# A split projection of 8192 rows: remaining columns by halves of K, and pairs of row tiles taken two at a time

## The chip, the cores and the metric

The kernel runs on one core of a Trainium2 chip. A core has five engines that run side by side, each with its own queue of instructions: TensorE (PE), which multiplies a stationary 128x128 tile with a moving one of up to 512 columns and adds up in PSUM; VectorE (DVE) and ScalarE (ACT), which read PSUM and write SBUF; GpSimd (POOL), which works on SBUF; and SyncE (SP), which here only issues DMA transfers. Weight loads of PE are shown on a line of their own (PEld). The metric is the device time of one execution in microseconds; the median of several runs counts.

## The reference

```python
def setup_inputs():
    batch, seq, hidden = 16, 512, 768
    x = randn(batch, seq, hidden); w_qkv = randn(hidden, 3 * hidden)      # float32

def reference(x, w_qkv):
    qkv = np.matmul(x, w_qkv)
    q, k, v = the three blocks of 768 columns
    return np.stack([q, k, v], axis=0).astype(np.float32)
```

So a matrix of 8192 x 768 is multiplied with one of 768 x 2304, and the result is stored as three matrices of 8192 x 768, in all 75.5 MB.

## The kernel before

**Tiling.** The rows are taken in 32 pairs of row tiles, p = 0 to 31, of 256 rows each (two tiles of 128). K is 768, split in two halves of 384, each three steps of 128 (`KH` = 3). Of the 2304 columns, 2048 are two column blocks of 1024, q = 0 and q = 1, and 256 are left, columns 1024 to 1279: these are "the remaining columns", `REM`.

**Quads.** A pair p and a block q make a quad: a product of 256 x 768 by 768 x 1024, seen as 2 x 2 by 2 x 2 blocks. It is computed with seven block products instead of eight (Strassen's scheme in Winograd's form). `product` (L233 to L247) issues one of them as three matmuls of 512 columns. Products 1 and 2 take x rounded to bfloat16 (`xb`) and weights in bfloat16 (`b1`). Products 3 to 7 take sums of blocks of x (`s`) and of the weights (`t`, `b22`) in float32r. `do` (L255 to L282) issues a product and what follows it. Product 1 starts the bank u.x, and ACT copies it to the output tile (L253). Product 2 goes to a bank of its own, u.z, and DVE adds it to that copy (L266). Product 6 is added to u.x and copied by ACT (L269). Product 5 starts the bank u.y. Product 7 is added to u.x, ACT copies it (L275) and DVE adds u.y (L276). Product 4 is added to u.x and copied by ACT (L279). Product 3 is added to u.y, and DVE adds that to an output block (L282). So u.x lives from product 1 to product 4, and u.y from product 5 to product 3. PSUM has eight banks, from one pool.

**The remaining columns.** `rem_row` (L297) issues six matmuls of 256 columns for one row tile, over all six steps of K, with x and weights in bfloat16 (`w_rem[0]` for the first half of K, `w_rem[1]` for the second). `rem` does both row tiles of a pair in one bank, and returns a function that has ACT copy the bank (L313), which returns one that stores it from SP (L314).

**Preparing x.** `load_x` loads a pair with four DMAs, two by SP and two by the queue it is given. `transpose` (L148) turns it on DVE, in one instruction of 128x1536 or in `parts`. `round_x` makes `xb` on POOL (L191), and `sums_x` makes the five blocks of `s` on POOL (L211 to L215). `ahead(p)` does the three in that order. The pools hold 3 loaded pairs, 2 transposed, 4 rounded, 2 of sums, 5 output tiles (of 128x2048, two row tiles by one block), and one more output-sized tile, "both", which the startup uses for weights and then for the quad of p = 2, q = 1.

**Startup.** For p = 0 and 1 everything is plain bfloat16 products (`block`), while the weights arrive. Between the second block and the first quad come the remaining columns of p = 0 and 1, the first four row tiles (`rems = [rem(p) for p in range(2)]`, L529). Their weights come with two DMAs from POOL (L419), one for each half of K, that round float32 to bfloat16 on the way. ACT's order there is: two copies of block results, rounding of the first row tile of p = 2 (L200), copy of p = 0's remainder (L313), two more block results (L446), rounding of the second row tile (L200), copy of p = 1's remainder (L313), then the copy of product 1 of the quad p = 2, q = 0 (L253). p = 2's quads follow, the first of them among the blocks.

**Steady part.** From p = 3 to 30 each pair is one call of `two(a, b, early)`, whose order is written out by hand: product 1 of both quads; `early`, which prepares p + 1 and loads p + 2; the pair's remainder; product 2 of both; then products 6, 6, 5, 7, 5, 7 of a, b, a, a, b, b, then 4 and 3 of a, its store, 4 and 3 of b, its store. A store of a quad is two DMAs on SP of 768 KB and 256 KB (L289, L290, L293, L294). The load of p + 2 goes half through SP and, from p = 5 on, half through ACT's queue.

**Last pair.** `last` takes p = 31 and stores by blocks of columns as they are ready (`store_cols`, L354), nine DMAs on SP and three on ACT. The first row tile's remainder comes after a's product 4, the second one's at the very end, each stored by ACT's queue (L370).

Instructions of an engine run in the order in which the program gives them. The framework adds the semaphore waits; a tile of a pool is handed out again when all that used it are done.

Of the kernel before, what the change touches and what calls it, by code (L numbers as in the profile page):

```python
# [10 lines left out]
def kernel(  # L11
# [20 lines left out]
    nc = tc.nc  # L32
    P = 128
    G = 32
# [5 lines left out]
    KH = KT // 2  # L40
    KC = K // 4
    NP = M // (2 * P)
    CB = 512
    REM = N3 - 4 * CB
    Q_OFF = (0, 2 * CB + REM)
    R_OFF = 2 * CB
    fp32 = mybir.dt.float32
# [13 lines left out]
    bt_pool = ctx.enter_context(tc.tile_pool(name="bt", bufs=1))  # L61
# [9 lines left out]
    ps_pool = ctx.enter_context(tc.tile_pool(name="ps", bufs=8, space=bass.MemoryType.PSUM))  # L71
# [5 lines left out]
    w_rem = [w_pool.tile([P, KH, REM], bf16, name="w_rem0"), None]  # L77
# [6 lines left out]
    both = bt_pool.tile([P, 2, KH * CB], fp32, name="both", tag="both")  # L84
# [37 lines left out]
    xin, xf, xb, sr = {}, {}, {}, {}  # L122
# [19 lines left out]
    def load_x(p, other):  # L142
        xin[p] = xin_pool.tile([P, 2 * P // G, KC], fp32, name="xin")
        load_x_half(p, 0, nc.sync)
        if other is not None:
            load_x_half(p, 1, other)

    def transpose(p, parts=1):  # L148
        t = xf_pool.tile([P, KT, 2 * P], fp32, name="xf")
        turned = t[:].rearrange("p j (g b) -> p g j b", b=G)  # L150
        rows = xin.pop(p)[:].rearrange("p g (a j) -> p g j a", a=G)
        n = 2 * P // G // parts
        for g in range(0, 2 * P // G, n):
            nc.vector.transpose(turned[:, g:g + n], rows[:, g:g + n])  # L154
        xf[p] = t

# [30 lines left out]
    def round_x(p):  # L189
        xb[p] = xb_pool.tile([P, KT, 2 * P], bf16, name="xb", tag="xb")  # L190
        nc.gpsimd.tensor_copy(out=xb[p][:], in_=xf[p][:])  # L191
# [12 lines left out]
    def sums_x(p, eng=None):  # L204
        t = xf.pop(p)
        a11, a12 = t[:, :KH, :P], t[:, KH:, :P]
        a21, a22 = t[:, :KH, P:], t[:, KH:, P:]
        s = s_pool.tile([P, 5, KH, P], f32r, name="s")
        sr[p] = s
        sums = {  # L210
            1: lambda g: g.tensor_tensor(s[:, 1], a21, a22, op=add),  # L211
            2: lambda g: g.tensor_tensor(s[:, 2], s[:, 1], a11, op=sub),  # L212
            3: lambda g: g.tensor_tensor(s[:, 3], a11, a21, op=sub),  # L213
            0: lambda g: g.tensor_copy(out=s[:, 0], in_=a22),
            4: lambda g: g.tensor_tensor(s[:, 4], a12, s[:, 2], op=sub),  # L215
        }
        if eng is not None:
            return sums
        for n in (1, 2, 3, 0, 4):
            sums[n](nc.gpsimd)  # L220
# [5 lines left out]
    def quad(p, q, pool=o_pool, tag="o"):  # L226
        u = Quad()
        u.p, u.q = p, q
        u.o = pool.tile([P, 2, 2 * CB], fp32, name="o", tag=tag)
        u.x = u.y = u.z = None  # L230
        return u
# [17 lines left out]
    def bank():  # L249
        return ps_pool.tile([P, CB], fp32, name="ps")  # L250

    def evacuate(u):
        nc.scalar.activation(u.o[:, 0, :CB], u.x[:], ident)  # L253

    def do(u, n, out=True):  # L255
        c11, c12 = u.o[:, 0, :CB], u.o[:, 0, CB:]
        c21, c22 = u.o[:, 1, :CB], u.o[:, 1, CB:]
        if n == 1:
            u.x = bank()
            product(u, 1, u.x, True)  # L260
            if out:
                evacuate(u)
        elif n == 2:
            u.z = bank()
            product(u, 2, u.z, True)
            nc.vector.tensor_tensor(c11, c11, u.z[:], op=add)  # L266
        elif n == 6:
            product(u, 6, u.x, False)
            nc.scalar.activation(c12, u.x[:], ident)  # L269
        elif n == 5:  # L270
            u.y = bank()
            product(u, 5, u.y, True)
        elif n == 7:
            product(u, 7, u.x, False)
            nc.scalar.activation(c22, u.x[:], ident)  # L275
            nc.vector.tensor_tensor(c22, c22, u.y[:], op=add)  # L276
        elif n == 4:
            product(u, 4, u.x, False)
            nc.scalar.activation(c21, u.x[:], ident)  # L279
        elif n == 3:  # L280
            product(u, 3, u.y, False)
            nc.vector.tensor_tensor(c12, c12, u.y[:], op=add)  # L282
# [4 lines left out]
    def store_quad(u):  # L287
        if u.q == 0:
            nc.sync.dma_start(rows_of(0, u.p, 0, H), u.o[:, :, :H])  # L289
            nc.sync.dma_start(rows_of(1, u.p, 0, 2 * CB - H), u.o[:, :, H:])  # L290
        else:
            part = 2 * H - Q_OFF[1]
            nc.sync.dma_start(rows_of(1, u.p, H - part, H), u.o[:, :, :part])  # L293
            nc.sync.dma_start(rows_of(2, u.p, 0, H), u.o[:, :, part:])  # L294


    def rem_row(p, r, ps):  # L297
        for j in range(KT):
            nc.tensor.matmul(  # L299
                ps, xb[p][:, j, r * P:(r + 1) * P], w_rem[j // KH][:, j % KH, :],  # L300
                start=(j == 0), stop=(j == KT - 1), skip_group_check=True,
            )

    def rem(p, eng=nc.sync, between=None):
        ps = ps_pool.tile([P, 2, REM], fp32, name="ps")
        rem_row(p, 0, ps[:, 0, :])
        if between is not None:
            between()
        rem_row(p, 1, ps[:, 1, :])

        def copied():
            o = or_pool.tile([P, 2, REM], fp32, name="orem")
            act.activation(o[:], ps[:], ident)  # L313
            return lambda: eng.dma_start(rows_of(1, p, R_OFF - H, R_OFF - H + REM), o[:])  # L314

        return copied

    def two(a, b, early, u=None):

        do(a, 1)  # L320
        do(b, 1, u is None)
        if u is None:
            early()
            rem(a.p)()()
        else:
            middle(u)
            copied = rem(a.p, between=lambda: third(u))
            evacuate(b)
            early()
            copied()()  # L330
            fourth(u)
        do(a, 2)
        do(b, 2)
        do(a, 6)
        do(b, 6)
        do(a, 5)
        do(a, 7)
        do(b, 5)
        do(b, 7)
        do(a, 4)  # L340
        do(a, 3)
        store_quad(a)
        do(b, 4)
        do(b, 3)
        store_quad(b)

    def store_cols(u, r, lo, hi, eng):

        c = Q_OFF[u.q] + lo
        end = Q_OFF[u.q] + hi  # L350
        while c < end:
            n = min(end, (c // H + 1) * H)
            row = (2 * u.p + r) * P
            eng.dma_start(  # L354
                out_flat[c // H, row:row + P, c % H:c % H + n - c],
                u.o[:, r, c - Q_OFF[u.q]:n - Q_OFF[u.q]],
            )
            c = n

    def last(a, b):  # L360

        p = a.p

        def rem_stored(r):
            ps = bank()
            rem_row(p, r, ps[:, :REM])
            o = or_pool.tile([P, 2, REM], fp32, name="orem")
            nc.scalar.activation(o[:, 0, :], ps[:, :REM], ident)  # L368
            row = (2 * p + r) * P
            nc.scalar.dma_start(out_flat[1, row:row + P, R_OFF - H:R_OFF - H + REM], o[:, 0, :])  # L370

        do(a, 1)
        do(b, 1)
        do(a, 2)
        do(a, 6)
        do(b, 2)
        do(b, 6)
        for u in (a, b):
            store_cols(u, 0, 0, CB, nc.sync)
        for u in (a, b):  # L380
            do(u, 5)
            do(u, 7)
            store_cols(u, 1, CB, 2 * CB, nc.sync)
        do(a, 4)
        store_cols(a, 1, 0, CB, nc.scalar)
        rem_stored(0)
        do(b, 4)
        store_cols(b, 1, 0, CB, nc.scalar)
        for u in (a, b):
            do(u, 3)  # L390
            store_cols(u, 0, CB, 2 * CB, nc.sync)
        rem_stored(1)


    ND = 2
# [21 lines left out]
    for h in range(2):  # L417
        rows = w_qkv.rearrange("(p j) n -> p j n", j=KT)[:, h * KH:(h + 1) * KH]
# [17 lines left out]
    quads = {}  # L436
# [49 lines left out]
    def ahead(p):  # L486
        transpose(p)
        round_x(p)
        sums_x(p)
# [7 lines left out]
    turned = [turn_row(0, 0)]  # L497
# [28 lines left out]
    late = block(  # L526
        0, 1, bt, [((j, ), range(4)) for j in range(KH)] + [(range(KH, KT), range(4))]
    )
    rems = [rem(p) for p in range(2)]  # L529
    transpose(2, 2)  # L530

    late[0]()
# [22 lines left out]
    u = quad(2, 0)  # L555
# [42 lines left out]
    u2 = quad(2, 1, bt_pool, "both")  # L598
    do(u2, 1)
    do(u2, 2)  # L600

    for p in range(ND + 1, NP):
        def early():
            if p + 1 < NP:
                ahead(p + 1)
            if p + 2 < NP:
                load_x(p + 2, nc.sync if p <= ND + 2 else nc.scalar)

        a, b = quad(p, 0), quad(p, 1)
        if p == ND + 1:  # L610
            two(a, b, early, u2)
        elif p < NP - 1:
            two(a, b, early)
        else:
            last(a, b)


# [28 lines left out]
```

## Time and profile before

| | us |
|---|---|
| median of 3 runs | 360.74 (360.47 to 361.23) |
| the profiled execution, its own time | 361.78 |
| its span, first to last instruction | 360.0 |
| PE idle before the first remainder on the second half of K, until the weights' DMA | 0.6 (by the page's ends of matmuls) |
| median from issue to landing, a quad's 768 KB store | 4.6 |
| the same, a quad's 256 KB store | 4.0 |
| the same, a load of x by SP / by ACT | 6.9 / 4.3 |

The span is that of one profiled execution, and what lies around it adds to its time. The granted clock of PE was 1.000 over the whole span. The DMA engines were busy for 90% and more of most slices of the span, at 299 GB/s on average. A line of the timeline has the start in us, the time that it spans, the engine, the source line, the operation, the tiles written and read, the shape, and the number of instructions merged; in brackets stands the idle time before it and what ended that.

### The profile page before, as it was taken

How to read it: one execution, taken by the hardware profiler on the slowest of the kernel's cores; microseconds unless marked ns; L12 is line 12 of the kernel's file. 1: busy time of each engine (PE TensorE's matmuls, PEld its weight loads, DVE VectorE, ACT ScalarE, POOL GpSimd, SP SyncE). 2: the span in 40 equal slices, each digit the busy share in tenths (PEclk: the TensorE clock that was granted, in tenths of full speed). 3: DMA queues.
4: the chain of work that ended last, by engine and by line, in shares of the span. 5: the costliest groups of instructions: out<-in, count | busy, mean ns of one | idle time of the engine just before them, and what ended most of it. 6: DMA issues, size and time to landing. Idle time of an engine off the chain costs nothing.

```text
span 360.0 us, 5248 instructions
## 1 busy us (share of the span) xinstructions
PE 351.5 (98%) x1749; PEld 251.4 (70%) x1780; DVE 227.8 (63%) x244; ACT 185.9 (52%) x316; POOL 178.8 (50%) x187
## 2 busy tenths in 40 slices
PE   7999999999999999999999999999999999999995
PEld 3465577777777777777777777777777777777764
DVE  2789676766566675566675566675556676556643
ACT  5469744545454545454545444455444445545443
POOL 0221856446664445665445665444665444665420
PEclk9999999999999999999999999999999999999999
DMA  7999999799998999899999899998999999989767
GB/s 265 340 367 345 325 357 371 236 333 298 275 325 301 295 276 290 282 319 301 292 285 284 284 309 309 292 285 282 290 295 315 293 295 272 297 283 322 291 238 257
DMA packets 82106, 107.73 MB, mean 299 GB/s; under 512 B 5408, under 2 KB 62240, under 8 KB 82080
## 3 DMA queue, kind: packets, MB, share of 16 engines
q1 hardware_dynamic: 66672, 96.35, 82.5%
q10 hardware_dynamic: 14608, 10.65, 8.9%
q0 software_dynamic: 800, 0.39, 0.8%
q8 instruction: 14, 0.23, 0.3%
q14 instruction: 12, 0.10, 0.1%
HBM read 32.28 MB, written 75.50 MB: 299 GB/s over the span
## 4 chain that ended last, share of the span: by engine, by line
PE 92%; DMA 5%; issue 1%; ACT 1%; ACTq 0%; POOL 0%; SPq 0%
PE ps L244 78%; PE ps L299 11%; PE ps L456 3%; DMA w_rem<-in_w_qkv_dram 2%; DMA xin<-in_x_dram 2%; DMA st<-in_w_qkv_dram 1%; ACT o L279 0%; ACTq L354 0%; POOL w_rem L419 0%; SPq L163 0%; ACT orem L368 0%; POOL mark L414 0%; ACTq L370 0%; ACTq L368 0%
## 5 line engine op out<-in xcount | busy, mean ns | idle before, releaser
L244 PE MATMUL ps<-t,s 128*128 128x512 f32 x720 | 181.2, 399 | 0.0
L244 PEld LDWEIGHTS ps<-t,s 128*128 128x128 f32 x720 | 135.0, 188 | 30.7
L191 POOL CAST xb<-xf 128x1536 bf16<-128x1536 f32 x28 | 41.0, 1464 | 132.2 <-DVE xf L154 132.2
L276 DVE TENSOR_TENSOR o<-o,ps 128x512 f32<-128x512 f32 x58 | 39.9, 688 | 91.5 <-ACT o L275 91.5
L154 DVE STREAM_TRANSPOSE xf<-xin 128x1536 f32<-128x1536 f32 (+1 forms) x32 | 88.7, 2775 | 1.7 <-DMA xin<-in_x_dram 1.7
L244 PE MATMUL ps<-b,xb 128*128 128x512 bf16 x331 | 85.3, 380 | 1.5
L244 PEld LDWEIGHTS <-xb 128*128 128x128 bf16 x360 | 32.8, 98 | 37.3 <-issue 7.6
L269 ACT ACTIVATE o<-ps 128x512 f32<-128x512 f32 x60 | 36.0, 600 | 43.6 <-PE ps L244 40.9
L275 ACT ACTIVATE o<-ps 128x512 f32<-128x512 f32 x58 | 34.7, 599 | 44.2 <-PE ps L244 44.2
L282 DVE TENSOR_TENSOR o<-o,ps 128x512 f32<-128x512 f32 x60 | 41.3, 688 | 21.4 <-PE ps L244 20.2
L244 PE MATMUL ps<-b,s 128*128 128x512 f32 x180 | 50.4, 389 | 0.0
L279 ACT ACTIVATE o<-ps 128x512 f32<-128x512 f32 x60 | 35.9, 598 | 24.6 <-PE ps L244 21.7
L253 ACT ACTIVATE o<-ps 128x512 f32<-128x512 f32 x60 | 35.8, 597 | 24.4 <-DVE o L282 20.7
L299 PE MATMUL ps<-w_rem,xb 128*128 128x256 bf16 x384 | 47.5, 273 | 0.6 <-DMA w_rem<-in_w_qkv_dram 0.6
L299 PEld LDWEIGHTS <-xb 128*128 128x128 bf16 x384 | 37.2, 98 | 12.3 <-issue 1.8
L266 DVE TENSOR_TENSOR o<-o,ps 128x512 f32<-128x512 f32 x60 | 37.8, 672 | 2.0 <-ACT o L253 1.3
L244 PEld LDWEIGHTS ps<-b,s 128*128 128x128 f32 x180 | 33.8, 188 | 7.1
L211 POOL TENSOR_TENSOR s<-xf 128x384 fp32r<-128x384 f32 x29 | 30.9, 1065 | 0.0
L212 POOL TENSOR_TENSOR s<-s,xf 128x384 fp32r<-128x384 f32 x29 | 29.4, 1015 | 2.3
L213 POOL TENSOR_TENSOR s<-xf 128x384 fp32r<-128x384 f32 x29 | 29.5, 1017 | 0.0
L215 POOL TENSOR_TENSOR s<-xf,s 128x384 fp32r<-128x384 f32 x29 | 29.5, 1017 | 0.0
L313 ACT ACTIVATE orem<-ps 128x512 f32<-128x512 f32 x31 | 18.5, 598 | 21.0 <-PE ps L299 21.0
(45 smaller groups left out, 119.3 us busy)
## 6 DMA issues: line engine op xcount, KB each, us to landing
out_dram<-o SPq DMA_DIRECT2D x62, 768.0 KB, 4.6
out_dram<-o SPq DMA_DIRECT2D x65, 256.0 KB, 4.0
xin<-in_x_dram SPq DMA_DIRECT2D x62, 192.0 KB, 6.9
xin<-in_x_dram ACTq DMA_DIRECT2D x50, 192.0 KB, 4.3
out_dram<-orem SPq DMA_DIRECT2D x31, 256.0 KB, 5.8
st<-in_w_qkv_dram SPq DMA_DIRECT2D x11, 256.0 KB, 5.6
st<-in_w_qkv_dram SPq DMA_DIRECT2D x3, 768.0 KB, 9.2
xin<-in_x_dram SPq DMA_DIRECT2D x4, 384.0 KB, 4.7
```

The lines of the kernel that those rows point to most:

```text
L154: nc.vector.transpose(turned[:, g:g + n], rows[:, g:g + n])
L191: nc.gpsimd.tensor_copy(out=xb[p][:], in_=xf[p][:])
L211: 1: lambda g: g.tensor_tensor(s[:, 1], a21, a22, op=add),
L244: nc.tensor.matmul(ps[:], lhs[j], rhs[j], start=(start and j == 0), stop=(j == KH - 1), skip_group_check=True,)
L253: nc.scalar.activation(u.o[:, 0, :CB], u.x[:], ident)
L266: nc.vector.tensor_tensor(c11, c11, u.z[:], op=add)
L269: nc.scalar.activation(c12, u.x[:], ident)
L275: nc.scalar.activation(c22, u.x[:], ident)
L276: nc.vector.tensor_tensor(c22, c22, u.y[:], op=add)
L279: nc.scalar.activation(c21, u.x[:], ident)
L282: nc.vector.tensor_tensor(c12, c12, u.y[:], op=add)
L299: nc.tensor.matmul(ps, xb[p][:, j, r * P:(r + 1) * P], w_rem[j // KH][:, j % KH, :], start=(j == 0), stop=(j == KT - 1), skip_group_check= ...
```

## The change

It has two parts and what they need.

**The remaining columns of p = 0 and 1 by halves of K.** A new function `rems_by_halves` takes two banks at once, and runs all four row tiles over the first half of K (12 matmuls), then all four over the second (12). The rest of `rem` is split off as `rem_copied`.

**Groups of two pairs from p = 6 on.** `group(p)` takes p and p + 1 together: product 1 of both quads of p, remainder of p, product 2 of both, then the same for p + 1, and only then products 3 to 7 of the quads of p (`rounded`, the second half of the former `two`), and those of p + 1. Preparation is placed by hand: `sums_x(p + 1)`, `transpose(p + 2)` and `round_x(p + 2)` after the first two products, `transpose(p + 3)` and `round_x(p + 3)` after the last product 2, `sums_x(p + 2)` after the first pair's float32r products. All loads of x go through SP. The first quad of a group takes the tile "both". In the last group the float32r products of p = 31 and its remainder are in `last`, which has lost its products 1 and 2.

**The way there.** For p = 3 to 5 `two` stays. Loads run further ahead (p = 3 loads 5 and 6, p = 4 loads 7, p = 5 loads 8 and 9), and in p = 5 the transpose for p = 7 is made in two halves that are put between the last products, followed by its rounding.

```diff
-    def transpose(p, parts=1):
+    def transpose(p, parts=1, split=False):
...
+        turns = [
+            lambda g=g: nc.vector.transpose(turned[:, g:g + n], rows[:, g:g + n])
+            for g in range(0, 2 * P // G, n)
+        ]
         xf[p] = t
+        if split:
+            return turns
+        for turn in turns:
+            turn()
...
+    def rems_by_halves(pairs):
+        banks = [ps_pool.tile([P, 2, REM], fp32, name="ps") for _ in pairs]
+        for h in range(2):
+            for p, ps in zip(pairs, banks):
+                for r in range(2):
+                    for j in range(KH):
+                        nc.tensor.matmul(
+                            ps[:, r, :], xb[p][:, h * KH + j, r * P:(r + 1) * P],
+                            w_rem[h][:, j, :], start=(h == 0 and r == 0 and j == 0),
+                            stop=(h == 1 and j == KH - 1), skip_group_check=True,
+                        )
+        return [rem_copied(p, ps) for p, ps in zip(pairs, banks)]
...
         do(a, 2)
         do(b, 2)
+        rounded(a, b, turns)
+
+    def rounded(a, b, turns=()):
+
         do(a, 6)
         do(b, 6)
         do(a, 5)
         do(a, 7)
         do(b, 5)
         do(b, 7)
+        for t in turns[:1]:
+            t()
         do(a, 4)
         do(a, 3)
         store_quad(a)
+        for t in turns[1:]:
+            t()
         do(b, 4)
         do(b, 3)
         store_quad(b)
...
-        do(a, 1)
-        do(b, 1)
-        do(a, 2)
-        do(a, 6)
-        do(b, 2)
-        do(b, 6)
         for u in (a, b):
             store_cols(u, 0, 0, CB, nc.sync)
+            do(u, 6)
...
-    rems = [rem(p) for p in range(2)]
+    rems = rems_by_halves(range(2))
...
+    def group(p):
+
+        quads = [quad(p, 0, bt_pool, "both"), quad(p, 1)]
+        do(quads[0], 1)
+        do(quads[1], 1)
+        sums_x(p + 1)
+        if p + 2 < NP:
+            transpose(p + 2)
+            round_x(p + 2)
+        if p + 4 < NP:
+            load_x(p + 4, nc.sync)
+        rem(p)()()
+        do(quads[0], 2)
+        do(quads[1], 2)
+        quads += [quad(p + 1, q) for q in range(2)]
+        do(quads[2], 1)
+        do(quads[3], 1)
+        if p + 5 < NP:
+            load_x(p + 5, nc.sync)
+        if p + 2 < NP:
+            rem(p + 1)()()
+        do(quads[2], 2)
+        do(quads[3], 2)
+        if p + 3 < NP:
+            transpose(p + 3)
+            round_x(p + 3)
+        rounded(*quads[:2])
+        if p + 2 < NP:
+            sums_x(p + 2)
+            rounded(*quads[2:])
+        else:
+            last(*quads[2:])
+
+    NG = ND + 4
+    extra = {NG - 3: (NG, ), NG - 1: (NG + 3, )}
+    for p in range(ND + 1, NG):
+        late_turns = []
+
         def early():
-            if p + 1 < NP:
-                ahead(p + 1)
-            if p + 2 < NP:
-                load_x(p + 2, nc.sync if p <= ND + 2 else nc.scalar)
...
+            ahead(p + 1)
+            for n in (p + 2 + (p > NG - 3), ) + extra.get(p, ()):
+                load_x(n, nc.sync)
+            if p == NG - 1:
+                late_turns.extend(transpose(NG + 1, 2, True))
+
+        two(quad(p, 0), quad(p, 1), early, u2 if p == ND + 1 else None, late_turns)
+        if p == NG - 1:
+            round_x(NG + 1)
+    for p in range(NG, NP, 2):
+        group(p)
```

More of the change, by code (lines that the diff above doesn't have):

```diff
@@ L152, in transpose @@
         n = 2 * P // G // parts
-        for g in range(0, 2 * P // G, n):
-            nc.vector.transpose(turned[:, g:g + n], rows[:, g:g + n])
+        turns = [
+            lambda g=g: nc.vector.transpose(turned[:, g:g + n], rows[:, g:g + n])
+            for g in range(0, 2 * P // G, n)
+        ]
         xf[p] = t
+        if split:
+            return turns
+        for turn in turns:
+            turn()
     def load_row(p, r):
@@ L309, in rem, with rem_copied @@
         rem_row(p, 1, ps[:, 1, :])
+        return rem_copied(p, ps, eng)
+    def rem_copied(p, ps, eng=nc.sync):
         def copied():
@@ L316, in rem, with two @@
         return copied
-    def two(a, b, early, u=None):
+    def rems_by_halves(pairs):
[10 more added lines that the diff above has]
+        return [rem_copied(p, ps) for p, ps in zip(pairs, banks)]
+    def two(a, b, early, u=None, turns=()):
         do(a, 1)
@@ L600 @@
     do(u2, 2)
-    for p in range(ND + 1, NP):
-        def early():
-            if p + 1 < NP:
-                ahead(p + 1)
-            if p + 2 < NP:
-                load_x(p + 2, nc.sync if p <= ND + 2 else nc.scalar)
[L609 to L615, printed above, removed]
+    def group(p):
[33 more added lines that the diff above has]
+        late_turns = []
+        def early():
+            ahead(p + 1)
[8 more added lines that the diff above has]
+        group(p)
 _INS = ['x', 'w_qkv']
```

## The prediction

> **What bounds the kernel now.** I read the page first: the span, the engines' busy time, and the chain that ended last.
>
> ```profile
> span 360.0 us, 5248 instructions
> ...
> PE 351.5 (98%) x1749; PEld 251.4 (70%) x1780; DVE 227.8 (63%) x244; ACT 185.9 (52%) x316; POOL 178.8 (50%) x187
> ...
> PE 92%; DMA 5%; issue 1%; ACT 1%; ACTq 0%; POOL 0%; SPq 0%
> ```
>
> TensorE (PE) is the bound, so the change can gain only where PE waits, where a matmul is slower than its neighbours, or before PE's first and after its last work. Next the chain in order of time, in the middle of the run.
>
> ```profile
> 111.94 9.16 PE ps L244 x40
> 121.10 1.31 PE ps L299 x12
> 122.68 9.16 PE ps L244 x40
> ```
>
> Pairs are counted from p = 0 to 31. A pair of row tiles takes 122.68 - 111.94 = 10.74 us, and PE has no idle time in it. What should it take? The timeline of PE gives the spacing of each sort of matmul (busy time less the last one's own, over the number less one, or start to start).
>
> ```profile
> 34.47 5.34 PE L456 MATMUL ps<-both,xb 128*128 128x512 bf16 x24
> ...
> 161.23 0.84 PE L244 MATMUL ps<-t,s 128*128 128x512 f32 x3
> 161.91 0.84 PE L244 MATMUL ps<-b,s 128*128 128x512 f32 x3
> ```
>
> bf16 of 512 columns: (5.34 - 0.38)/23 = 0.2157 us (0.38 is the mean of one). float32r: (161.91 - 161.23)/3 = 0.2267. bf16 of 256 columns, for the remaining columns: the startup rows below, (2.45 - 0.27)/20 = 0.109. A pair has 30, 12 and 12 of float32r, bf16-512 and bf16-256: 6.80 + 2.59 + 1.31 = 10.70. So 0.04 us of each 10.74 is lost, and it can only lie at the two changes of type, into float32r and out of it. That is what grouping can save.
>
> **Grouping, steady part.** The pairs p = 6 to 31 become 13 groups. Each saves one change into float32r and one out of it: 0.04 us. The last group saves two such rounds, because `last` also loses its alternation of products 2 and 6. 14 x 0.043 = -0.60 us. Bounds -0.5 to -0.7 from the rounding of the spacings.
>
> The rest of the group must stay hidden behind PE's 21.4 us. I place its work on a clock that starts with the group: bf16 work until 7.8 (four times 1.31 for products 1 and 2 with two remainders of 1.31), float32r of the first pair to 14.6, of the second to 21.4.
> - POOL: `sums_x(p+1)` needs only its buffer, free at 0; its five steps take 4.5 (1.0 each, the copy 0.5): done at 4.7, needed at 14.6. `round_x(p+2)` (1.46) 6.2, needed at 21.4. `round_x(p+3)` after the second transpose, 13.1, needed at 25. `sums_x(p+2)` from 14.7 to 19.3, needed at 29. Nothing here is near. If POOL's cover were gone each us past its time would cost PE a us per group; the nearest is 2 us away (19.3 against the next group's transpose into that buffer at 21.4+0.8).
> - DMA issues: the loads of x leave ACT's queue for SP's: eight loads, eight quad stores, two remainder stores per group. Rows give 0.4 to 1.2 us for an issue, so 7 to 22 us of 21.4; the loads land far ahead (issued by 12, first read at 22). Behind a blocked SP issue wait only stores, whose buffers are written again 5 us or more after landing. Cost 0.
> - Output buffers: three of five are used per group and "both" for the first quad; "both" is stored at about 14.3 and 15, lands in the 4.6 us of its row, and is written at 22. Cost 0.
> - VectorE (DVE) is the tight one:
>
> ```profile
> 152.65 2.94 DVE L154 STREAM_TRANSPOSE xf<-xin 128x1536 f32<-128x1536 f32 x1
> 155.51 1.25 DVE L266 TENSOR_TENSOR o<-o,ps 128x512 f32<-128x512 f32 x2
> 159.34 0.69 DVE L276 TENSOR_TENSOR o<-o,ps 128x512 f32<-128x512 f32 x1 [2.58 <-ACT o L275]
> ```
>
> Now the transpose runs at the start of a pair, long before L276. In a group the second transpose comes after the fourth product 2, hence into the start of float32r work at 155.76 on this clock: the last L266 starts 0.22 after it (as L282 does after its matmul), the transpose at 0.83, L276 at 0.83 + 2.86 = 3.69 instead of 159.34 - 155.76 = 3.58. So L276 of the first quad is 0.11 us later; product 3 overwrites what it reads and its weight load is due at 4.56, L276 ends at 4.38. Slack about 0.15. Cost 0, with a rival below.
>
> **Into the groups.** In pair p = 5 the transpose for p = 7 is put in two halves (1.4 to 1.6 each) among the last products; the second ends some 9.3 after the float32r start, `round_x(7)` 1.5 later at 10.8, and PE wants it at 6.8 + 3.9 = 10.7. +0.1 us once, 0 to 0.3. The extra loads in p = 3 and p = 5 fall into a stretch in which DMA is 90% busy and delay stores by 2 to 4 us; the buffer of p = 3's first quad is next written 10 us after its store. Cost 0.
>
> **The remainders by halves.** The startup on PE and on ACT:
>
> ```profile
> 19.80 0.49 PE L299 MATMUL ps<-w_rem,xb 128*128 128x256 bf16 x3
> 20.87 2.45 PE L299 MATMUL ps<-w_rem,xb 128*128 128x256 bf16 x21 [0.58 <-DMA w_rem<-in_w_qkv_dram]
> ```
>
> ```profile
> 22.05 0.60 ACT L313 ACTIVATE orem<-ps 128x512 f32<-128x512 f32 x1 [0.60 <-PE ps L299]
> 22.55 1.08 ACT L446 ACTIVATE o<-ps 128x512 f32<-128x512 f32 x2
> 23.50 0.86 ACT L200 ACTIVATE xb<-xf 128x768 bf16<-128x768 f32 x1
> 24.23 0.61 ACT L313 ACTIVATE orem<-ps 128x512 f32<-128x512 f32 x1
> 24.71 0.62 ACT L253 ACTIVATE o<-ps 128x512 f32<-128x512 f32 x1
> ```
>
> Three matmuls use the first half of the weights, then PE waits until 20.87 for the second: 20.87 - 19.80 - 3 x 0.109 = 0.74 us. With 12 matmuls on the first half PE gets to the second at 21.11, after it landed: the wait is gone. But ACT then works without a gap from 22.05 to L253's end, 25.33, and the first float32r product (25.77 now) must not start before L253 has read its bank. The first pair's remainder ends only 0.09 earlier (21.11 + 0.65 = 21.76 against 21.85), so L253 ends at 25.24; with the release and a float32r weight load of 0.19, PE starts at 25.53. Gain 0.24, and 0.5 is moved into a wait for ACT. Bounds 0 and -0.74; I take -0.24 since L253 is the next thing late. After that DVE, ACT and POOL have half a us or more in hand at each row that PE follows. (The Trainium skill, "TensorE: Matmul & The Clock Gate", Architectural detail, says that a matmul can begin before its weight load completes; by it the 0.19 falls away and the gain is 0.43. The page of the profile has 188 ns for such a load and shows no start from standstill, so it is open.)
>
> **The end.** This term speaks against the change. Bytes in the last stretch:
>
> ```profile
> 345.60:352.00 6.40, 6.40 (x30) 4.48 (x29) 2.47 (x4) 2.99 (x5) 0.00 (x0) 1.00 1.03 397
> 352.00:354.30 2.30, 2.30 (x15) 1.77 (x14) 0.74 (x2) 1.58 (x3) 0.00 (x0) 1.00 0.45 156
> 354.30:358.70 4.40, 1.85 (x12) 1.14 (x10) 1.37 (x2) 0.98 (x2) 0.00 (x0) 1.00 0.97 355
> ...
> DMA packets 3104, 4.46 MB, mean 262 GB/s; under 512 B 288, under 2 KB 2080, under 8 KB 3104
> ```
>
> The last two numbers of a row are the DMA share and GB/s. From 343 on, 4.46 MB are stored: the quads of p = 30 and all of p = 31. They begin at 345.6, 1.8 us after p = 30's first quad has its product 3 (343.8), and pause around 353 because PE has not made more; the last matmul streams until 355.97, the last bytes leave at 358.7, 2.7 later. In the changed kernel products 1 and 2 of p = 31 and their 2.6 us lie before those stores, not between: from that product 3 to PE's end are 6 + 30 float32r and 12 small matmuls, 8.16 + 1.31 = 9.47 us, so bytes begin 7.67 before the end. At 397 GB/s 4.46 MB take 11.23: they end 3.56 after PE, 0.9 later than now. Bounds: 410 GB/s, the most in a busy window of this trace, +0.5; 355 throughout, +2.2. I take +0.9, the rate of the window most like it. (ACT issues 0.79 MB of these. By the Trainium skill, "DMA: Bandwidth & Descriptors", Issuing engines are not separate DMA queues, they share the engines with SP's; the trace agrees, 355 with both at work. Otherwise 3.67 MB would end 1.6 after PE, the term would be 0 and the time 360.0.)
>
> **Sum.** -0.60 - 0.24 + 0.1 + 0.9 = +0.16 us. The profiled execution took 361.78 (span 360.0 and 1.78 around it), 1.04 above the median of the runs, 360.74. It becomes 361.94; the median 360.9. A measurement of this kernel can tell about 0.2%, 0.72 us, from no change: below 360.02 is faster, above 361.46 slower.
>
> **Rivals.**
> - *Product 3 waits for DVE in each group* (slower). Place: L276 of the first quad; price (delay - 0.15) x 13; it decides once the second transpose starts over 1 us into the float32r work. Half an addition late (0.35) makes 0.2 x 13 = 2.6: 363.5. For: only 0.15 us in hand. Against: POOL beside a transpose doesn't stretch it (1.58 us for a half with and without POOL at work in the startup), and its buffer is free 4 us ahead.
> - *The end drains at 355 GB/s*: +1.3 on the forecast, 362.2. For: both queues and 1 KB rows give that now. Against: most of the backlog is 3 KB rows.
> - *Startup gives all 0.74 and the end costs 0 to 0.5* (faster): -0.6 - 0.74 + 0.1 + 0 to 0.5 = -1.2 to -0.7, 359.5 to 360.0. For: the w_rem wait does vanish. Against: ACT's gapless chain, and bytes that have to move.
> - *It does not do what it says*: eight PSUM banks, of which four are held by products 1; if the third product 2 got the bank that a remainder still holds, PE would wait 0.8 a group (ACT's copy of 0.6 and its release), 13 x 0.8 = +10, 371. Against: in a pair now product 2 follows a remainder without a wait, so another bank is handed out.
>
> **How the numbers follow.** Forecast 0.50, faster rival 0.19, drain 0.13, DVE 0.15, banks 0.03. So same 0.50, faster 0.19, slower 0.31. The range, 360.0 to 362.6, holds the forecast, the drain and the near parts of the DVE case and of the faster one; the forecast's own is 360.2 to 361.4.
>
> **What would show it.** Steady groups of 21.44 us; no PE idle for w_rem, but one before the first float32r product; DMA share near 1 from PE's end less 7.7 to its end plus 3.6. Wrong would be any idle time of PE that repeats each 21.4 us, or a last landing as soon after PE as now.

## The result and the profile after

| | before | after |
|---|---|---|
| median of 6 runs, us | 360.99 (360.47 to 361.75) | 362.58 (362.3 to 362.9) |
| ratio after / before, 95% interval | | 1.0041 (1.003 to 1.0052) |
| profiled execution, us | 361.78 | 362.9 |
| its span, us | 360.0 | 361.1 |

The changed kernel is 0.41% slower, 1.1 to 1.9 us by the interval. The page of the changed kernel, in the same three lines as before:

```profile
span 361.1 us, 5246 instructions
...
PE 353.5 (98%) x1780; PEld 252.2 (70%) x1780; DVE 230.9 (64%) x245; ACT 186.1 (52%) x316; POOL 178.4 (49%) x187
...
PE 94%; DMA 3%; ACT 1%; SPq 0%; issue 0%; ACTq 0%
```

PE is still the bound, so the answer lies again in the three stretches of the prediction. The steady part, in the chain of the changed kernel (start, us, what; a group is counted here from its first remainder, 1.31 us):

```profile
185.20 1.31 PE ps L305 x12
186.51 2.59 PE ps L250 x12
189.10 1.31 PE ps L305 x12
190.41 16.26 PE ps L250 x72
206.67 1.31 PE ps L305 x12
```

206.67 - 185.20 = 21.47 us for a group, where two pairs took 21.48 and 21.44 was forecast. Nearly the whole gain of grouping is missing, with PE working without a gap. DVE in the same group shows what is late (L272 and L282 are the former L266 and L276):

```profile
191.15 1.34 DVE L272 TENSOR_TENSOR o<-o,ps 128x512 f32<-128x512 f32 x2 [2.47 <-PE ps L250]
192.40 3.07 DVE L154 STREAM_TRANSPOSE xf<-xin 128x1536 f32<-128x1536 f32 x1
195.41 0.63 DVE L282 TENSOR_TENSOR o<-o,ps 128x512 f32<-128x512 f32 x1
```

The float32r work of this group starts at 191.54 (its second matmul's start less one spacing; the first one's record begins earlier, while the last bfloat16 matmul still runs). The transpose starts 0.86 after that and lasts 3.07, not 2.94, so L282 ends at 4.50 instead of the 4.38 worked out. Product 3 has to wait for it. Its weight load, due at 4.56, starts at 4.61, 0.12 after L282's end (196.036 to 196.152 in the trace):

```profile
196.15 0.60 PEld L250 LDWEIGHTS ps<-b,s 128*128 128x128 f32 x3
```

From there six float32r matmuls follow each other at 0.228 to 0.236 us instead of 0.227, in all 0.03 us more. These are slower matmuls and no idle time. The other slow stretch of a group is at its change from bfloat16 to float32r, where the first matmuls lose 0.025 us, as they do in each pair of the kernel before; the change back costs 0.003. This is most of the 0.04 us that the prediction put there.

The startup of the changed kernel, on PE, and what PE waited for between 24 and 26 us (waiting engine and line, releaser, us in total, times, longest):

```profile
19.70 2.78 PE L333 MATMUL ps<-w_rem,xb 128*128 128x256 bf16 x24
...
25.29 1.65 PE L250 MATMUL ps<-t,s 128*128 128x512 f32 x6
```

```profile
PEld ps L250 <- ACT o L259: 0.4, 1, 0.4
PEld L305 <- ACT xb L206: 0.2, 1, 0.2
```

The wait for w_rem is gone: all 24 matmuls run in one stretch. In its place PE waits 0.4 us for L259, the copy that the prediction named (L253 before), and 0.2 for the rounding of the second row tile. From the first remainder to the first float32r product it is now 25.29 - 19.70 = 5.59 us, before 25.69 - 19.80 = 5.89. To the second float32r matmul it is 5.92 and before 6.20.

The end (the last two numbers are the DMA share and GB/s), and the instruction traffic from 343 us on:

```profile
347.80:354.00 6.20, 6.20 (x32) 4.96 (x31) 1.85 (x3) 3.37 (x6) 0.00 (x0) 1.00 1.03 397
354.00:359.40 5.40, 1.72 (x11) 1.04 (x9) 1.37 (x2) 0.98 (x2) 0.00 (x0) 0.85 1.03 371
359.40:361.10 1.70, 0.00 (x0) 0.00 (x0) 0.00 (x0) 0.00 (x0) 0.00 (x0) 0.50 0.01 2
...
q14 instruction: 1, 0.01, 0.1%
```

PE's last matmul starts at 355.45 and is counted to 355.56, one spacing later. The DMA engines are full from 347.8 on without a pause, and the last bytes leave at 359.56: 4.0 us after PE, before 2.7. From there to the end of the span it takes another 1.56, before 1.26. A q14 line, instruction memory being loaded, was not there in the same stretch of the kernel before.

From the first float32r product to the end of the span the changed kernel takes 361.1 - 25.3 = 335.8 us, the kernel before 360.0 - 25.7 = 334.3. The loss of 1.5 us lies there. The end alone has 4.0 - 2.7 + 1.56 - 1.26 = 1.6, so what lies between gives nothing in sum.

### The profile page after: what moved, and what is told of

Same layout as the page of the kernel before. It is cut to its first block, busy times and chain, and to the rows that moved or that the text cites. A ratio compares the mean times of both kernels' runs of the same rounds, so it can differ in the third digit from the quotient of the medians.

```text
span 361.1 us, 5246 instructions
## 1 busy us (share of the span) xinstructions
PE 353.5 (98%) x1780; PEld 252.2 (70%) x1780; DVE 230.9 (64%) x245; ACT 186.1 (52%) x316; POOL 178.4 (49%) x187
## 4 chain that ended last, share of the span: by engine, by line
PE 94%; DMA 3%; ACT 1%; SPq 0%; issue 0%; ACTq 0%
PE ps L250 78%; PE ps L305 10%; PE ps L481 6%; DMA xin<-in_x_dram 2%; DMA out_dram<-o 1%; PE ps L333 1%; SPq L169 0%; ACT orem L322 0%; ACT o L471 0%; ACT xb L206 0%; ACT o L285 0%; PE ps L190 0%; ACT xc L173 0%; ACT o L259 0%; ACT orem L398 0%
## 5 line engine op out<-in xcount | busy, mean ns | idle before, releaser
L250 PE MATMUL ps<-t,s 128*128 128x512 f32 x720 | 178.2, 395 | 0.1
L250 PEld LDWEIGHTS ps<-t,s 128*128 128x128 f32 x720 | 134.9, 188 | 30.1 <-ACT o L259 0.4
L154 DVE STREAM_TRANSPOSE xf<-xin 128x1536 f32<-128x1536 f32 (+1 forms) x33 | 91.0, 2760 | 1.9 <-DMA xin<-in_x_dram 1.9
L250 PE MATMUL ps<-b,xb 128*128 128x512 bf16 x360 | 85.3, 380 | 0.0
L282 DVE TENSOR_TENSOR o<-o,ps 128x512 f32<-128x512 f32 x58 | 39.4, 679 | 60.0 <-ACT o L281 60.0
L250 PEld LDWEIGHTS <-xb 128*128 128x128 bf16 x360 | 33.9, 98 | 37.1 <-issue 4.2
L272 DVE TENSOR_TENSOR o<-o,ps 128x512 f32<-128x512 f32 x60 | 38.8, 678 | 31.1 <-PE ps L250 17.4
L259 ACT ACTIVATE o<-ps 128x512 f32<-128x512 f32 x60 | 35.8, 597 | 32.0 <-PE ps L250 17.4
L250 PE MATMUL ps<-b,s 128*128 128x512 f32 x180 | 50.6, 390 | 0.0
L305 PE MATMUL ps<-w_rem,xb 128*128 128x256 bf16 x360 | 44.6, 273 | 0.0
L305 PEld LDWEIGHTS <-xb 128*128 128x128 bf16 x360 | 34.8, 98 | 11.2 <-issue 0.8
L250 PEld LDWEIGHTS ps<-b,s 128*128 128x128 f32 x180 | 33.7, 188 | 7.3
```

The costliest lines, as they stand in the source:

```text
L154: lambda g=g: nc.vector.transpose(turned[:, g:g + n], rows[:, g:g + n])
L250: nc.tensor.matmul(ps[:], lhs[j], rhs[j], start=(start and j == 0), stop=(j == KH - 1), skip_group_check=True,)
L305: nc.tensor.matmul(ps, xb[p][:, j, r * P:(r + 1) * P], w_rem[j // KH][:, j % KH, :], start=(j == 0), stop=(j == KT - 1), skip_group_check= ...
```

## The experiments

Times are medians against the kernel before on the same chip; the ratio is what counts, since the kernel before itself has 360.99 to 361.4 us from one set of runs to the next.

**The startup part alone.** The kernel before with `rems_by_halves`:

```diff
-    rems = [rem(p) for p in range(2)]
+    rems = rems_by_halves(range(2))
```

> The kernel before with the first part of the change alone. If the wait for the second half of the remainders' weights is what is saved and ACT's chain keeps the rest of it, the first float32r product starts 0.24 to 0.40 us earlier than in the kernel before (25.69 in its profile) and the time falls by as much: about 360.7. Rival: ACT's chain, or a startup that differs from run to run, takes all of it: no change, 361.0.

Measured 360.94 against 361.4, ratio 0.999 (0.9981 to 0.9999). The first float32r product came at 24.69, a whole microsecond earlier, but the first remainder had come 0.63 earlier too, which the change can't do: the time up to there differs from run to run. Between the two marks it took 5.53 us. The same in the other kernels of this study that have this startup gives 5.49 to 5.64; the kernel before has 5.88 and, in a second profile, 5.98. So the part is worth 0.2 to 0.5 us by these profiles, 0.4 in the middle, about half of the wait that it removes (0.74 in one profile and 0.82 in the other).

**A second profile of the kernel before**, for that comparison.

> The kernel before once more, for a second profile. If the startup takes another time in each run, its first float32r product is not at 25.69 us again but some tenths from it, the pairs take 10.74 us and the last bytes leave 2.7 us after PE's last matmul as before; all theories expect the same here.

The first float32r product was at 25.50, the pairs took 10.74 us, and the last bytes left 2.71 us after PE. 361.57 us in its one run.

**The second transpose earlier.** The changed kernel with one block moved ahead of the last two products 2:

```diff
+        if p + 3 < NP:
+            transpose(p + 3)
+            round_x(p + 3)
         if p + 2 < NP:
             rem(p + 1)()()
         do(quads[2], 2)
         do(quads[3], 2)
-        if p + 3 < NP:
-            transpose(p + 3)
-            round_x(p + 3)
```

> The changed kernel with the second transpose of a group put ahead of its last two products 2. If DVE's lateness at the first quad's product 3 makes the second slow stretch of float32r matmuls, that stretch is gone and a steady group takes 21.44 us instead of 21.467 (two of twelve 21.50): 0.03 to 0.05 us a group, 0.4 us in all, 362.2. Rival: POOL's rounding, which starts 0.57 us before the stretch, makes it; it now runs at the start of the float32r work, the loss moves there, a group stays at 21.47 and the time at 362.6.

The chain of this kernel, then DVE in a later group (with the weight load of product 3) and in the very first group:

```profile
185.79 1.31 PE ps L305 x12
187.10 2.59 PE ps L250 x12
189.69 1.31 PE ps L305 x12
191.00 16.23 PE ps L250 x72
207.23 1.31 PE ps L305 x12
```

```profile
192.08 1.25 DVE L272 TENSOR_TENSOR o<-o,ps 128x512 f32<-128x512 f32 x2
195.71 0.69 DVE L282 TENSOR_TENSOR o<-o,ps 128x512 f32<-128x512 f32 x1 [2.38 <-ACT o L281]
196.70 0.64 PEld L250 LDWEIGHTS ps<-b,s 128*128 128x128 f32 x3
```

```profile
81.98 1.25 DVE L272 TENSOR_TENSOR o<-o,ps 128x512 f32<-128x512 f32 x2
84.67 3.10 DVE L154 STREAM_TRANSPOSE xf<-xin 128x1536 f32<-128x1536 f32 x1 [1.43 <-POOL s L221]
87.69 1.24 DVE L272 TENSOR_TENSOR o<-o,ps 128x512 f32<-128x512 f32 x2
```

A steady group takes 207.23 - 185.79 = 21.44 us, the forecast of the prediction to 0.01, and L282 now waits for ACT (the bracket) with DVE idle before it. The weight load of product 3 starts when it is due, 4.56 us into the float32r work. The rival fell: the rounding now starts 0.09 us into that work instead of 3.99, and no loss came with it, since the first matmuls there lose 0.026 us, against 0.025 without it. But the kernel as a whole got no faster: 363.5, ratio 1.0059 (1.0047 to 1.0072), and from the first float32r product to the end of the span 336.2 us against 335.8. The expectation overlooked the first group. There the transposes of the pair before it are still in DVE's queue, the buffer is not free, the early transpose waits 1.43 us for POOL, and the additions behind it come late at product 3: that group lost 0.8 us, more than the eleven others gained.

**The rounding alone, put later.** As a check on the same rival, only `round_x(p + 3)` was put behind `rounded(*quads[:2])`.

> The changed kernel with only POOL's rounding of p + 3 put behind the first pair's float32r products. If DVE's lateness makes the second slow stretch, it stays where it is, at the first quad's product 3 (4.56 us into the float32r work), with no rounding near it; a group takes 21.47. Rival, POOL: the stretch is gone from there and appears 0.57 us after the rounding's new start, some 7 us into the float32r work.

A group took 21.47 us as before, and the slow stretch stayed where product 3 of the first quad begins (one run, 362.59 us). But the rounding stayed too. POOL has no other work between the old place and the new one, so it still rounds as soon as the transpose is done, 4.04 us into the float32r work against 3.99. This run therefore says nothing about the rival. What speaks against POOL is the kernel above, where the rounding did move, and the next one, where it keeps its place and the loss follows L282.

**DVE later still.** Four small fills behind the second transpose:

```diff
             transpose(p + 3)
             round_x(p + 3)
+            pad = m_pool.tile([P, 96], fp32, name="pad")
+            for _ in range(4):
+                nc.vector.memset(pad[:], 0.0)
```

> The changed kernel with four small DVE fills behind the second transpose of each group, which make DVE 0.4 to 0.7 us later at the first quad's product 3; nothing of the computation changes. If PE waits there and has no slack left, each group grows by that delay, to 21.9 to 22.2 us. Rival, the recorded slack of 0.15 us is there and the stretch has another cause: the group grows by 0.25 to 0.55.

DVE and PE in one group of it:

```profile
129.94 3.07 DVE L154 STREAM_TRANSPOSE xf<-xin 128x1536 f32<-128x1536 f32 x1
132.99 0.81 DVE L655 MEMSET pad<- 128x96 f32 x4
133.72 1.22 DVE L282 TENSOR_TENSOR o<-o,ps 128x512 f32<-128x512 f32 x2
```

```profile
128.90 5.13 PE L250 MATMUL ps<-t,s 128*128 128x512 f32 x21
134.49 0.93 PE L250 MATMUL ps<-b,s 128*128 128x512 f32 x3 [0.46 <-DVE o L282]
```

The fills put L282 0.77 us later, and the group takes 22.17 to 22.21 us, 0.70 to 0.74 more; the one run took 372.09 us. Now PE stands idle in front of product 3 (L250 with `b`), released by L282. The rounding still starts at 3.99, and from L282's end to the weight load it takes 0.12 again. So the changed kernel had next to no slack at that place: of 0.77 us of delay, 0.70 to 0.74 are lost in each group.

**The last two pairs one at a time.** The changed kernel with groups up to p = 29 and the old end:

```diff
-    for p in range(NG, NP, 2):
+    for p in range(NG, NP - 2, 2):
         group(p)
+    p = NP - 2
+    two(quad(p, 0), quad(p, 1), lambda: sums_x(p + 1))
+    last(quad(p + 1, 0), quad(p + 1, 1))
```

(with products 1 and 2 back in `last`.)

> The changed kernel with the last two pairs taken one at a time, as in the kernel before (p = 30 with its stores before products 1 and 2 of p = 31). If the bytes stored at the end are the cost, the last bytes leave 2.7 us after PE's last matmul instead of 3.9, and the time falls by 1.1 to 1.5: about 361.2. Rival, the loss is in the steady groups: no more than 0.1 of it comes back, 362.5.

Measured 362.01, ratio 1.0016 (1.0007 to 1.0025): 0.9 us of the loss came back, less than expected. The last bytes left 3.2 us after PE, not 2.7, and the rest to the end took 1.77 instead of 1.26, with the same stores as in the kernel before. Here too instruction memory was loaded in the last microseconds. In this run every group had the longer loss at product 3, 21.50 us.

**A group of the last two pairs alone.** The counterpart, `NG = NP - 2` in the changed kernel, with loads past p = 31 left out.

> The changed kernel with pairs up to p = 29 and a group of p = 30 and 31 alone. If the end is what made the change slower, this has all of its cost and none of the other groups': last bytes 3.9 us after PE's last matmul against 2.7, time 1.2 to 1.5 above the startup part alone, ratio to the kernel before 1.003. Rival, the 13 groups make the loss: ratio 0.999.

Measured 362.01 against 361.12, ratio 1.0026 (1.0016 to 1.0037). Its last stretch:

```profile
347.10:358.90 11.80, 8.24 (x43) 6.29 (x41) 3.43 (x5) 4.37 (x9) 0.00 (x0) 1.00 1.01 378
358.90:360.30 1.40, 0.00 (x0) 0.00 (x0) 0.00 (x0) 0.00 (x0) 0.00 (x0) 0.57 0.00 0
```

The last bytes left 3.69 us after PE, 0.97 later than in the kernel before, and the rest took 1.45, 0.2 more. No instruction block was loaded there, though here too all loads go through SP. So the stores alone cost 1.16 us, and the interval holds that less the 0.4 of the startup. The rival, that the 13 groups make the loss, fell: this kernel has only one and keeps most of it.

**The mended groups.** Earlier transpose in all groups but the first, and the last two pairs one at a time.

> The changed kernel with the second transpose earlier in all groups but the first, and the last two pairs one at a time. If the two losses are DVE's lateness and the stores at the end, steady groups take 21.44 us, the last bytes leave 2.7 to 3.2 us after PE's last matmul, and the time is that of the kernel before less 0.36 for the startup, less 0.04 x 10 for the groups, plus 0.1 on the way into them: 0.6 less, ratio 0.998. Rival: groups cost something else as well, and the ratio is no lower than that of the startup part alone, 0.999.

Groups took 21.44 us, but the ratio was 1.0013 (1.0004 to 1.0022): a miss. The end again: last bytes 3.19 after PE and 1.78 to the end. Instruction traffic from 341 us on:

```profile
q8 instruction: 1, 0.02, 0.4%
q14 instruction: 2, 0.02, 0.3%
```

The first of the two q14 blocks, of 8 KB each, is loaded 1.4 us before the last bytes, the second 1.5 us after them. The kernel before this one with the last two pairs one at a time has the same two.

**The same with ACT's loads back.** All that differs is who issues half of each load of x:

```diff
-            load_x(p + 4, nc.sync)
+            load_x(p + 4, nc.scalar)
...
-            load_x(p + 5, nc.sync)
+            load_x(p + 5, nc.scalar)
```

> The mended groups with half of each load of x issued by ACT again, as in the kernel before. If an 8 KB instruction block that is fetched on a DMA engine during the last stores (as SP's longer list of issues makes it fall there) costs 0.5 us of the last bytes and 0.5 after them, it falls elsewhere now: last bytes 2.7 us after PE's last matmul and 1.3 to the end, 1.0 less than the mended groups, ratio to the kernel before 0.998. Rival: the fetch stays in the end, or is not the cause, and the last bytes leave 3.2 us after PE's last matmul; ratio 1.001.

Measured 360.39 against 361.17, ratio 0.9979 (0.997 to 0.9988). The last bytes left 2.72 us after PE, 1.26 before the end, as in the kernel before. The same view of this kernel from 341 us on has no q14 any more:

```profile
DMA packets 3105, 4.47 MB, mean 256 GB/s; under 512 B 288, under 2 KB 2080, under 8 KB 3104
...
q8 instruction: 1, 0.02, 0.4%
```

So this version is 0.2% faster than the kernel before, and faster than the changed kernel. The 0.5 us of the last bytes and the 0.5 us after them went with the q14 blocks. All six kernels of this study with such a block among their last stores have the last bytes later than their counterparts without one (3.19 against 2.72 us after PE, or 3.94 to 4.02 against 3.69 where the last two pairs are grouped). SP's loads alone do not do it, since the group of the last two pairs has them and no block. How a block delays the end is not shown. Until PE's last matmul the two mended kernels issue their last stores within 0.03 us of each other. After it, ACT issues its last store 0.25 us later, and SP's last one lands 3.41 instead of 2.85 us after that matmul's start, though it was issued only 0.03 later. Which engine's instructions they are was not measured.

**The startup part once more**, beside it.

> The first part of the change alone once more, beside the one above: ratio 0.999, last bytes 2.7 us after PE's last matmul; all theories expect the same.

360.93 against 361.17, ratio 0.9994 (0.9985 to 1.0002), last bytes 2.72 us after PE. Its gain is near what can be told apart. The groups add 0.5 us to it by the medians, with intervals that overlap a little; in the profiles the stretch from the remainder of p = 4 to that of p = 30 takes 278.89 us with the groups and 279.24 without.

## Why the prediction was right or wrong

The range held the time, 362.58, by 0.02 us at its upper edge, and that is luck. The likeliest case, no change with +0.16 us, did not come. The upper part of the range was there for stores that drain at 355 GB/s and for a late DVE; the stores ran at 381, the late DVE cost 0.03 us a group, and most of the loss came from the end, part of it from something that no rival named. The rivals on the slower side had 0.31. By steps:

- **Grouping, -0.60.** The step that failed. PE's 0.04 us a pair do go with the grouping: steady groups of 21.44 appeared as soon as DVE was out of the way. In the changed kernel they took 21.45 to 21.50. The term measured -0.1 over the twelve groups that end before the last one begins. What failed is the sentence "Slack about 0.15. Cost 0". The transpose took 3.07 instead of 2.94 (why is open; POOL did nothing beside it), and the chain of three DVE instructions ended 0.12 later than worked out. The 0.06 that were left were less than the 0.12 from L282's end to the weight load, a step that the working left out. The rival named the place, the instruction and the direction; its threshold (a transpose starting over 1 us into the float32r work) was too generous, since the loss was there at 0.86. The sign that was to show it, idle time of PE that repeats, did not appear: the loss was in slower matmuls.
- **Into the groups, +0.1.** Right: the first group took 21.57, 0.10 more than a steady 21.47, and PE waited where it was expected to, for the rounding of p = 7.
- **The remainders by halves, -0.24.** The mechanism was right, the wait for w_rem went and a wait for ACT's copy took its place; the size was -0.30 in the changed kernel's profile and -0.4 in the middle of all. ACT's copy ended no earlier than before, counted from the first remainder. But from the copy's end to the second float32r matmul it took 0.39 (the weight load began after 0.05, the matmul came 0.34 later), where the forecast comes to 0.1 + 0.19 + 0.23 = 0.52 with one spacing more. The sentence of the Trainium skill ("TensorE: Matmul & The Clock Gate", Architectural detail) that a matmul can begin before its weight load completes gave 0.43. The trace agrees in part: the second matmul came 0.08 sooner than a whole load and a spacing allow, and no row shows the first one's start by itself.
- **The end, +0.9.** The bytes were right: +0.97 in the kernel that groups only the last two pairs, where they began 7.68 us before PE's end and ran at 392 GB/s. But the end costs 1.6 in the changed kernel. 0.2 more comes after the last bytes (why is open), and about 0.4 goes with an instruction block loaded among the last stores, of which the profile before gave no sign. The sharing of the DMA engines by SP's and ACT's queues was right (371 GB/s with both at work); with engines of its own for ACT the term would have been 0.
- **Loads moved to SP, 0.** Right for the steady part, wrong for the end: with half of them back on ACT's queue the instruction load was gone from the last stores, and 1.0 us with it, between the two mended kernels.
- **The banks.** That rival fell; no product 2 waited.

Together: -0.3 + 0.1 - 0.1 + 1.6 = +1.3 us, inside the interval of 1.1 to 1.9. The two profiled spans differ by 1.16, since the first remainder came 0.1 earlier in the changed kernel, and the medians by 1.6.

## What to carry to other kernels

When stores run at the full rate of the DMA engines, count the bytes that are left when the last compute begins: compute that is moved ahead of the last stores takes away time in which they could drain. Here 2.6 us were moved, and the last bytes left 0.97 later. A release has to come before the waiting engine needs it by the time that passes from one to the other, here 0.12 us from DVE's end to the weight load, so a step that costs nothing "because there is slack" should have that slack measured by delaying it, which takes one run. And a gain that fails to come may still be there: moving one instruction brought it back.

## What the runs showed of the hardware

- float32r matmuls of 512 columns follow each other at 0.227 us and bf16 ones at 0.216; after a change to float32r a run of some six of them loses 0.025 us, after a late release 0.03.
- A weight load that waited for a DVE addition started 0.12 us after its end; one that waited for an ACT copy in the startup, 0.05 us.
- 8 KB blocks of instructions, one loaded while the last stores ran and one after them, went with 0.5 us more to the last bytes and 0.5 us more after them.
- Kernels with the same startup had their first float32r product between 24.28 and 25.78 us; only differences within one run, from a mark near by, could be used there.
